# A running log-sum-exp in which the fp16 matmuls become fp32 row sums, PSUM-held carries and a checked fast path

## The chip, the cores and the metric

The kernel runs on one core of a Trainium2 chip. The metric is the device time of one execution in microseconds, as the median of several runs; 3 runs of the kernel before gave a median of 1262.75 us (1262.56 to 1262.97). The profile is one more execution, recorded instruction by instruction.

## The reference

```
B, S, D = 4, 4096, 4128
x = np.random.randn(B, S, D).astype(np.float32)

out[:, 0, :] = x[:, 0, :]
for t in range(1, S):
    mx = np.maximum(out[:, t-1, :], x[:, t, :])
    out[:, t, :] = mx + np.log(np.exp(out[:, t-1, :] - mx) + np.exp(x[:, t, :] - mx))
```

For every batch and column it is the logarithm of the running sum of exp(x) down the 4096 rows. Both kernels compute exp, a running sum, and the logarithm of it.

## The kernel before, in words

**Tiles.** A step takes 128 x r consecutive rows of one batch, all 4128 columns, as one tile `xt` with r consecutive rows on each of the 128 partitions. r is 3 (`R`), and 2 in one step of each batch (first in batch 0, last in the others): 11 steps per batch, 44 in all, 40 of them with r = 3. A tile of r = 3 is 6192 KB. Four tiles are in rotation (`bufs = 4`). `Step.load` (L132) and `Step.store` (L135) both issue on SP's queue: after the store of step s comes the load of step s + 3, which has to wait until the tile's previous content is stored.

**Chunks.** A step is cut into four chunks of 1024 columns (`CH`); the last one also has the 32 columns that are left. For each chunk:

- `exp` (L147, ScalarE) writes exp(x) as fp16 over the chunk.
- `later` (L155, VectorE) adds rows 1 and 2 of each partition into `sum`, as fp32r.
- `head` (TensorE) makes row 0 of each partition in a PSUM tile `pt`: the triangle `incl` times row 0 of all partitions, the strict triangle `excl_r` times `sum` (L167), and `pick` times the carry of the step before. A matmul has 512 columns (`MM`), so each is there twice.
- `stage(j)` takes the logarithm of `pt` for row j (L198, ScalarE), and then adds row j + 1 into `pt` by a matmul with the identity `ident`. The rows of one chunk run one after another; three chunks are at different stages at the same time, with three `pt` tiles.
- `keep` (L111, L112, VectorE), after the last row, writes the last 32 partitions of `pt` as two fp16 parts, the rounded value and the remainder, into `carry`. `pick` adds both parts of partition 127 in the next step.

The 32 left columns go the same way with a small tile `qt` and `carry_t` (`tail_head`, L203). `mm` records a matmul, at L97 where the weights change and at L101 where they are those of the matmul before; the built order has a weight load ahead of both.

**Order.** The whole schedule is written out by hand (`manual_schedule`): the loop over chunks at L229 gives `later` of the next chunk, then the stages of three chunks, the store at a step's end, `exp` two chunks ahead and `head` one chunk ahead. Each engine runs its instructions in the order in which they are written.

Of the kernel before, what the change touches and what calls it, by code (L numbers as in the profile page):

```python
# [6 lines left out]

FP32 = mybir.dt.float32
FP16 = mybir.dt.float16
FP32R = mybir.dt.float32r  # L10
ACT = mybir.ActivationFunctionType
P = 128
R = 3
CH = 1024
MM = 512
HI, LO = 96, 32


def _constants(nc, pool):


    def tri(base, name):
        t = pool.tile([P, P], FP16, name=name)
        nc.gpsimd.memset(t, 1.0)

        nc.gpsimd.affine_select(
            out=t, in_=t, pattern=[[1, P]], compare_op=mybir.AluOpType.is_ge,
            fill=0.0, base=base, channel_multiplier=-1,
        )
        return t  # L30

    def ones_where_zero(bases, step, name):
        t = pool.tile([P, P], FP16, name=name)
        nc.gpsimd.memset(t, 0.0)
        for base in bases:
            nc.gpsimd.affine_select(
                out=t, in_=t, pattern=[[step, P]], compare_op=mybir.AluOpType.not_equal,
                fill=1.0, base=base, channel_multiplier=1,
            )
        return t  # L40

    return (
        tri(0, "incl"),
        tri(-1, "excl"),
        ones_where_zero([0], -1, "ident"),
        ones_where_zero([-(HI + 31), -(LO + 31)], 0, "pick"),
    )


@with_exitstack  # L50
def kernel(
    ctx: ExitStack,
    tc: tile.TileContext,
    x: bass.AP,
    out: bass.AP,
):

    nc = tc.nc
    B, S, D = x.shape
    assert S % P == 0
    n_main = D // CH
    tail = D - n_main * CH
    t0 = n_main * CH
    last = n_main - 1

    nc.scalar.preload_act_table_set("natural_log_exp_and_others")
    consts = ctx.enter_context(tc.tile_pool(name="consts", bufs=1))
    incl, excl, ident, pick = _constants(nc, consts)

    bufs = 4
    xpool = ctx.enter_context(tc.tile_pool(name="xpool", bufs=bufs))
    cpool = ctx.enter_context(tc.tile_pool(name="cpool", bufs=1))
    pmain = ctx.enter_context(tc.tile_pool(name="pmain", bufs=3, space=bass.MemoryType.PSUM))
    ptail = ctx.enter_context(tc.tile_pool(name="ptail", bufs=2, space=bass.MemoryType.PSUM))

    carry = [cpool.tile([P, CH], FP16, name=f"carry{c}") for c in range(n_main)]
    carry_t = cpool.tile([P, tail], FP16, name="carry_t")
    for t in (*carry, carry_t):
        nc.vector.memset(t, 0.0)

    spool = ctx.enter_context(tc.tile_pool(name="spool", bufs=1))
    excl_r = consts.tile([P, P], FP32R, name="excl_r")
    nc.vector.tensor_copy(excl_r, excl)

    ctx.enter_context(tc.manual_schedule())  # L90

    held = [None]

    def mm(pt, w, rhs, start=False, stop=False):

        if held[0] is not w:
            nc.tensor.matmul(pt, lhsT=w, rhs=rhs, start=start, stop=stop, skip_group_check=True)  # L97
            held[0] = w
            return
        pe = nc.tensor  # L100
        pe.add_instruction(mybir.InstMatmult(  # L101
            name=nc.get_next_instruction_name(),
            ins=[pe.lower_ap(rhs), pe.lower_ap(w, for_matmul_weights=True)],
            outs=[pe.lower_ap(pt, opt=True)],
            start_tensor_calc=start, stop_tensor_calc=stop, ldweights=False,
            tile_size=(P, P), tile_position=(0, 0), bass_skip_group_check=True,
        ))

    def keep(cr, pt):

        nc.vector.tensor_copy(cr[HI:HI + 32, :], pt[HI:HI + 32])  # L111
        nc.vector.tensor_tensor(  # L112
            out=cr[LO:LO + 32, :], in0=pt[HI:HI + 32], in1=cr[HI:HI + 32, :],
            op=mybir.AluOpType.subtract,
        )

    class Step:


        def __init__(self, b, row, r):  # L120
            self.b, self.row, self.r = b, row, r
            self.first = row == 0

        def dram(self, t):
            rows = t[self.b, self.row:self.row + P * self.r, :]
# [2 lines left out]
        def load(self):  # L128
            full = xpool.tile([P, R, D], FP32, name="xt")
            self.xt = full[:, :self.r, :]  # L130
            self.half = self.xt.bitcast(FP16)
            nc.sync.dma_start(out=self.xt, in_=self.dram(x))  # L132

        def store(self):
# [2 lines left out]
    class Chunk:  # L137
        def __init__(self, step, c):
            self.t, self.c = step, c
            self.w = D - last * CH if c == last else CH  # L140

        def e(self, j, a, b):
            return self.t.half[:, j, 2 * self.c * CH + a:2 * self.c * CH + b]

        def exp(self):
            c0, w = self.c * CH, self.w
            nc.scalar.activation(  # L147
                self.t.half[:, :, 2 * c0:2 * c0 + w], self.t.xt[:, :, c0:c0 + w], ACT.Exp,
            )

        def later(self):

            if self.t.r == 3:
                self.sum = spool.tile([P, CH], FP32R, name="sum")
                nc.vector.tensor_tensor(  # L155
                    out=self.sum, in0=self.e(1, 0, CH), in1=self.e(2, 0, CH),
                    op=mybir.AluOpType.add,
                )

        def head(self):  # L160
            t = self.t
            pt = self.pt = pmain.tile([P, CH], FP32, name="pt")
            for s in range(0, CH, MM):
                mm(pt[:, s:s + MM], incl, self.e(0, s, s + MM), start=True)
            if t.r == 3:
                for s in range(0, CH, MM):
                    nc.tensor.matmul(  # L167
                        pt[:, s:s + MM], lhsT=excl_r, rhs=self.sum[:, s:s + MM],
                        start=False, stop=False, skip_group_check=True,
                    )  # L170
                held[0] = None
            else:
                for s in range(0, CH, MM):
                    mm(pt[:, s:s + MM], excl, self.e(1, s, s + MM))
            if not t.first:
                for s in range(0, CH, MM):
                    mm(pt[:, s:s + MM], pick, carry[self.c][:, s:s + MM])
            if self.c == last:
                self.tail_head()

        def tail_head(self):


            t, r = self.t, self.t.r
            full = ptail.tile([P, R, tail], FP32, name="qt")
            qt = self.qt = full[:, :r, :]
            to = lambda v, n: v.unsqueeze(1).to_broadcast([P, n, tail])
            for i in range(r):
                mm(qt[:, i:, :], incl, to(self.e(i, CH, CH + tail), r - i), start=i == 0)
            for i in range(1, r):  # L190
                mm(qt[:, :i, :], excl, to(self.e(i, CH, CH + tail), i))
            if not t.first:
                mm(qt, pick, to(carry_t, r))

        def stage(self, j):

            t, c, pt = self.t, self.c, self.pt
            nc.scalar.activation(t.xt[:, j, c * CH:(c + 1) * CH], pt, ACT.Ln)  # L198
            if j + 1 < t.r:
                for s in range(0, CH, MM):  # L200
                    mm(pt[:, s:s + MM], ident, self.e(j + 1, s, s + MM), stop=j + 2 == t.r)
                if c == last and j == 0:
                    nc.scalar.activation(t.xt[:, :, t0:D], self.qt, ACT.Ln)  # L203
                    keep(carry_t, self.qt[:, t.r - 1, :])
            else:
                keep(carry[c], pt)

    steps = []
    for b in range(B):
        n = S // P  # L210
# [3 lines left out]
        row = 0  # L214
# [2 lines left out]
            row += P * r  # L217
        assert row == S

    chunks = [Chunk(s, c) for s in steps for c in range(n_main)]  # L220
    ahead = bufs - 1
    for s in steps[:bufs]:
        s.load()
    stored = 0
    chunks[0].exp()
    chunks[1].exp()
    chunks[0].later()
    chunks[0].head()
    for g in range(len(chunks) + R - 1):  # L229
        if g + 1 < len(chunks):  # L230
            chunks[g + 1].later()
        for d in range(R - 1, -1, -1):
            if 0 <= g - d < len(chunks) and d < chunks[g - d].t.r:
                k = chunks[g - d]
                k.stage(d)
                if k.c == last and d + 1 == k.t.r:
                    k.t.store()
                    if bufs <= stored + ahead < len(steps):
                        steps[stored + ahead].load()
                    stored += 1  # L240
        if g + 2 < len(chunks):
            chunks[g + 2].exp()
        if g + 1 < len(chunks):
            chunks[g + 1].head()


# [28 lines left out]
```

## Time and profile before

| | before |
|---|---|
| median of 3 runs | 1262.75 us |
| profiled execution, span from first to last instruction | 1261.5 us |
| TensorE busy, matmuls | 661.2 us, 52% |
| VectorE busy | 647.7 us, 51% |
| ScalarE busy | 947.3 us, 75% |
| DMA queue of loads and stores, share of 16 engines | 99.4% |
| moved, mean rate | 541.44 MB, 429 GB/s |
| mean granted TensorE clock | 0.722 |

Busy time is the time in which an engine has an instruction of the program running, as a share of the span. In the lists of groups a line names the source line, the engine, the operation, its output and inputs by the program's names with partitions x elements and type, and the number of instructions; after the first bar stand the busy time in us and the mean of one in ns, and after the second bar the idle time of the engine just before them and what ended most of it. PE is TensorE, PEld its weight loads, DVE VectorE, ACT ScalarE, POOL GpSimd, SP SyncE, whose queue issues the DMAs. The rows of tenths cut the span into 40 slices: 9 is 90% or more; PEclk is the clock that TensorE was granted, in tenths of full speed.

### The profile page before, as it was taken

The page shows a single profiled execution, that of the slowest core. Times are in us where ns is not written, and L with a number is a line of the kernel's source. Part 1 is how long each engine was busy: PE and PEld are TensorE (multiplying, and loading weights), DVE is VectorE, ACT ScalarE, POOL GpSimd, SP SyncE. Part 2 cuts the span into 40 slices and gives each one's busy share as a digit, 9 for nine tenths or more (in the row PEclk, how much of TensorE's full clock was granted, in tenths as well). Part 3 has the DMA queues.
Part 4 walks back from the last instruction along what each step waited for, and adds up shares of the span by engine and source line. Part 5 has one row for each costly group of instructions (what it writes and reads, how often), then busy time and mean ns, then how long its engine had stood idle before and what let it go on. Part 6 is the DMA issues. An engine that isn't in the chain of part 4 may idle for free. (4 is left out here: it accounts for less than half of the span.)

```text
span 1261.5 us, 5926 instructions
## 1 busy us (share of the span) xinstructions
PE 661.2 (52%) x1948; PEld 236.7 (19%) x1948; DVE 647.7 (51%) x606; ACT 947.3 (75%) x733; POOL 2.2 (0%) x13
## 2 busy tenths in 40 slices
PE   3655545465555555555446554555534655544562
PEld 1222111122121111211112121111111221111120
DVE  2674445554555545545446545544544645544454
ACT  5997777777777777778669777777866977777784
POOL 0000000000000000000000000000000000000000
PEclk9987676766577776768757677766775767787666
DMA  9999999999999999999999999999999999999998
GB/s 410 410 437 434 429 430 437 431 430 431 440 430 431 430 439 430 431 433 431 438 433 435 428 432 438 432 430 431 434 435 430 435 427 436 434 434 429 437 416 346
DMA packets 12702, 541.44 MB, mean 429 GB/s; under 512 B 1408, under 2 KB 1408, under 8 KB 1408
## 3 DMA queue, kind: packets, MB, share of 16 engines
q1 hardware_dynamic: 12672, 541.07, 99.4%
q8 instruction: 15, 0.25, 0.1%
q14 instruction: 15, 0.12, 0.0%
HBM read 270.53 MB, written 270.53 MB: 429 GB/s over the span
## 5 line engine op out<-in xcount | busy, mean ns | idle before, releaser
L147 ACT ACTIVATE xt<-xt 128x3072 f16<-128x3072 f32 (+3 forms) x176 | 478.3, 2717 | 248.4 <-DMA xt<-in_x_dram 248.4
L198 ACT ACTIVATE xt<-pt 128x1024 f32<-128x1024 f32 x512 | 487.5, 1029 | 2.5 <-PE pt L101 0.7
L155 DVE TENSOR_TENSOR sum<-xt 128x1024 fp32r<-128x1024 f16 x160 | 196.0, 1225 | 531.2 <-ACT xt L147 406.7
L97 PE MATMUL pt<-xt,ident 128*128 128x512 f16 x176 | 82.9, 471 | 482.8 <-ACT xt L198 482.8
L111 DVE CAST carry<-pt 32x1024 f16<-32x1024 f32 x176 | 216.4, 1230 | 46.4 <-ACT xt L198 41.3
L101 PE MATMUL pt<-xt,ident 128*128 128x512 f16 x496 | 209.5, 495 | 28.4 <-ACT xt L198 28.1
L112 DVE TENSOR_TENSOR carry<-pt,carry 32x1024 f16<-32x1024 f32 x176 | 215.9, 1226 | 6.1
L167 PE MATMUL pt<-sum,excl_r 128*128 128x512 f32 x320 | 198.7, 716 | 0.0
L101 PEld LDWEIGHTS <-ident 128*128 128x128 f16 x496 | 52.4, 106 | 646.5 <-issue 636.1
L97 PE MATMUL pt<-xt,incl 128*128 128x512 f16 x176 | 95.7, 544 | 71.7 <-DVE carry L112 54.0
L167 PEld LDWEIGHTS pt<-sum,excl_r 128*128 128x128 f32 x320 | 95.4, 298 | 48.4 <-issue 31.1
L101 PE MATMUL pt<-xt,incl 128*128 128x512 f16 x176 | 99.2, 564 | 0.0
L97 PE MATMUL pt<-carry,pick 128*128 128x512 f16 x160 | 84.4, 528 | 0.0
L101 PE MATMUL pt<-carry,pick 128*128 128x512 f16 x160 | 79.4, 496 | 0.0
L97 PEld LDWEIGHTS <-incl 128*128 128x128 f16 x220 | 23.7, 108 | 192.7 <-DVE carry L112 167.0
L203 ACT ACTIVATE xt<-qt 128x96 f32<-128x96 f32 (+1 forms) x44 | 10.9, 249 | 46.3 <-PE pt L101 46.3
L97 PEld LDWEIGHTS <-pick 128*128 128x128 f16 x200 | 24.2, 121 | 67.0 <-issue 66.3
L101 PEld LDWEIGHTS <-incl 128*128 128x128 f16 x260 | 27.6, 115 | 12.7 <-issue 9.2
L97 PEld LDWEIGHTS <-ident 128*128 128x128 f16 x176 | 21.4, 122 | 30.3 <-issue 24.3
L101 PEld LDWEIGHTS <-pick 128*128 128x128 f16 x160 | 20.5, 128 | 2.4 <-issue 1.7
L111 DVE CAST carry_t<-qt 32x32 f16<-32x32 f32 x44 | 8.7, 197 | 13.7 <-ACT xt L203 13.5
L97 PE MATMUL qt<-xt,incl 128*128 128x96 f16 (+1 forms) x44 | 10.6, 240 | 0.0
(25 smaller groups left out, 79.8 us busy)
## 6 DMA issues: line engine op xcount, KB each, us to landing
xt<-in_x_dram SPq DMA_DIRECT2D x40, 6192.0 KB, 42.3
out_dram<-xt SPq DMA_DIRECT2D x40, 6192.0 KB, 28.1
xt<-in_x_dram SPq DMA_DIRECT2D x4, 4128.0 KB, 37.4
out_dram<-xt SPq DMA_DIRECT2D x4, 4128.0 KB, 29.7
```

The costliest lines, as they stand in the source:

```text
L97: nc.tensor.matmul(pt, lhsT=w, rhs=rhs, start=start, stop=stop, skip_group_check=True)
L101: pe.add_instruction(mybir.InstMatmult(name=nc.get_next_instruction_name(), ins=[pe.lower_ap(rhs), pe.lower_ap(w, for_matmul_weights=True) ...
L111: nc.vector.tensor_copy(cr[HI:HI + 32, :], pt[HI:HI + 32])
L112: nc.vector.tensor_tensor(out=cr[LO:LO + 32, :], in0=pt[HI:HI + 32], in1=cr[HI:HI + 32, :], op=mybir.AluOpType.subtract,)
L147: nc.scalar.activation(self.t.half[:, :, 2 * c0:2 * c0 + w], self.t.xt[:, :, c0:c0 + w], ACT.Exp,)
L155: nc.vector.tensor_tensor(out=self.sum, in0=self.e(1, 0, CH), in1=self.e(2, 0, CH), op=mybir.AluOpType.add,)
L167: nc.tensor.matmul(pt[:, s:s + MM], lhsT=excl_r, rhs=self.sum[:, s:s + MM], start=False, stop=False, skip_group_check=True,)
L198: nc.scalar.activation(t.xt[:, j, c * CH:(c + 1) * CH], pt, ACT.Ln)
L203: nc.scalar.activation(t.xt[:, :, t0:D], self.qt, ACT.Ln)
```

## The change

- exp(x) stays fp32, in place. VectorE makes the running sums of the r rows on each partition, in place (`sums`, r - 1 additions).
- The columns are three chunks of 1024 and a last one of 1056. For each of the first three a PSUM tile `base[c]` stays for the whole kernel. `head` adds the strict triangle `excl` times the partitions' totals (the last row of `sums`), in fp32; VectorE adds `base[c]` to all r rows in one instruction (`add`); `pass_on` then starts the next step's base with `pick` times the last row, so the carry needs no copy. For the last chunk the base is made in three tiles of 352 columns (two in rotation), from `carry` and the totals, and added piece by piece (`add_rest`); `add` copies the last 32 partitions to `carry`.
- One logarithm per chunk, over all r rows, from SBUF (`ln`).
- A range check: `total` adds up the final sums of each batch and chunk on partitions 96 to 127, `first` holds exp(-x) of the first rows, and all of it is compared with 2^40. Every engine reads the flag and branches: if the check fails, `_general` computes everything again by the reference's own steps, 4095 of them in a loop.
- All fp16 and fp32r tiles, the identity, `later`, `stage`, `keep` and `tail_head` are gone. The order is still written by hand.

Lines in the text on the changed kernel are its own (L112 sums, L124 and L126 head of the last chunk, L131 head, L137 add_rest, L144 carry copy, L147 add, L155 pass_on, L108 exp, L167 ln, L163 total, L249 to L256 `_general`).

```diff
+BUFS = 4
+HI = 96
+LIMIT = float(2 ** 40)
...
+    carry = cpool.tile([P, rest], FP32, name="carry")
...
+    base = [pkeep.tile([P, CH], FP32, name=f"base{c}") for c in range(3)]
...
         def exp(self):
-            c0, w = self.c * CH, self.w
-            nc.scalar.activation(
-                self.t.half[:, :, 2 * c0:2 * c0 + w], self.t.xt[:, :, c0:c0 + w], ACT.Exp,
-            )
-
-        def later(self):
-
-            if self.t.r == 3:
-                self.sum = spool.tile([P, CH], FP32R, name="sum")
+            rows = self.rows(0, self.t.r)
+            nc.scalar.activation(rows, rows, ACT.Exp)
+
+        def sums(self):
+            for j in range(1, self.t.r):
                 nc.vector.tensor_tensor(
-                    out=self.sum, in0=self.e(1, 0, CH), in1=self.e(2, 0, CH),
-                    op=mybir.AluOpType.add,
-                )
+                    out=self.row(j), in0=self.row(j - 1), in1=self.row(j), op=ALU.add)
 
         def head(self):
             t = self.t
...
+            own = self.row(t.r - 1)
+            if self.end:
+                self.base = []
+                for s in range(0, rest, sub):
+                    q = prest.tile([P, MM], FP32, name="q")
+                    self.base.append(q)
+                    if not t.first:
+                        nc.tensor.matmul(q[:, :sub], lhsT=pick, rhs=carry[:, s:s + sub],
+                                         start=True, stop=False, skip_group_check=True)
+                    nc.tensor.matmul(q[:, :sub], lhsT=excl, rhs=own[:, s:s + sub],
+                                     start=t.first, stop=True, skip_group_check=True)
+                    self.add_rest(s, q)
             else:
                 for s in range(0, CH, MM):
...
+                    nc.tensor.matmul(base[self.c][:, s:s + MM], lhsT=excl, rhs=own[:, s:s + MM],
+                                     start=t.first, stop=True, skip_group_check=True)
+
+        def add_rest(self, s, q):
+            t = self.t
+            rows = t.xt[:, :, self.a + s:self.a + s + sub]
+            nc.vector.tensor_tensor(
+                out=rows, in0=rows, in1=q[:, :sub].unsqueeze(1).to_broadcast([P, t.r, sub]),
+                op=ALU.add)
+
+        def add(self):
+            t = self.t
+            if self.end:
+                nc.vector.tensor_copy(carry[HI:P, :], self.row(t.r - 1)[HI:P])
+                return
+            rows = self.rows(0, t.r)
+            nc.vector.tensor_tensor(
+                out=rows, in0=rows, in1=base[self.c].unsqueeze(1).to_broadcast([P, t.r, CH]),
+                op=ALU.add)
+
+        def pass_on(self):
+            if self.end:
+                return
+            for s in range(0, CH, MM):
+                nc.tensor.matmul(base[self.c][:, s:s + MM], lhsT=pick,
+                                 rhs=self.row(self.t.r - 1)[:, s:s + MM],
+                                 start=True, stop=False, skip_group_check=True)
+
+        def total(self):
+            own = carry if self.end else base[self.c]
+            i = 4 * self.t.b + self.c
+            nc.vector.tensor_reduce(
+                out=part[HI:P, i:i + 1], in_=own[HI:P, :self.w], axis=AX.X, op=ALU.add)
+
+        def ln(self):
+            rows = self.rows(0, self.t.r)
+            nc.scalar.activation(rows, rows, ACT.Ln)
...
     chunks[0].exp()
     chunks[1].exp()
-    chunks[0].later()
+    chunks[0].sums()
     chunks[0].head()
...
+    for g, k in enumerate(chunks):
+        if not k.end:
+            chunks[g + 1].sums()
+        k.add()
+        k.pass_on()
+        if g + 2 < n:
             chunks[g + 2].exp()
...
+        k.ln()
+        if g and chunks[g - 1].t.last:
+            chunks[g - 1].total()
...
+        if k.end:
+            k.t.store()
+            if BUFS <= stored + BUFS - 1 < len(steps):
+                steps[stored + BUFS - 1].load()
+            stored += 1
+            if g + 1 < n:
+                chunks[g + 1].sums()
+        if g + 1 < n:
             chunks[g + 1].head()
+
+    chunks[-1].total()
+    nc.vector.tensor_reduce(out=every, in_=part, axis=AX.X, op=ALU.add)
+    q = prest.tile([P, MM], FP32, name="q")
+    nc.tensor.matmul(q[:1, :1], lhsT=every, rhs=ones, start=True, stop=True)
+    nc.vector.tensor_scalar(out=flag, in0=q[:1, :1], scalar1=LIMIT, scalar2=None, op0=ALU.is_le)
...
+    with ExitStack() as inner:
+        _fast(inner, tc, x, out, flag)
+    good = nc.values_load(flag, min_val=0, max_val=1, skip_runtime_bounds_check_because="a comparison gives 0 or 1")
+    with tc.If(good == 0, preferred_fallthrough_block=False):
+        with ExitStack() as inner:
+            _general(inner, tc, x, out)
```

## The prediction

> **What bounds the kernel now.** I read the page from the top: the busy shares, then the queues, then the costliest groups, and after them the timeline of TensorE. The first two say that no engine is full and the one DMA queue is.
>
> ```profile
> PE 661.2 (52%) x1948; PEld 236.7 (19%) x1948; DVE 647.7 (51%) x606; ACT 947.3 (75%) x733; POOL 2.2 (0%) x13
> ...
> PEclk9987676766577776768757677766775767787666
> DMA  9999999999999999999999999999999999999998
> ...
> q1 hardware_dynamic: 12672, 541.07, 99.4%
> ```
>
> 99.4% of 1261.5 us is 1254 us of transfers. The work is 40 steps of three row blocks and 4 steps of two, 42.7 three-block steps, so a full step has 1254 / 42.7 = 29.4 us. A change that leaves the bytes alone costs nothing while each step's work stays under that. The groups give the prices (mean ns of one stands after the bar).
>
> ```profile
> L147 ACT ACTIVATE xt<-xt 128x3072 f16<-128x3072 f32 (+3 forms) x176 | 478.3, 2717 | 248.4 <-DMA xt<-in_x_dram 248.4
> L155 DVE TENSOR_TENSOR sum<-xt 128x1024 fp32r<-128x1024 f16 x160 | 196.0, 1225 | 531.2 <-ACT xt L147 406.7
> L111 DVE CAST carry<-pt 32x1024 f16<-32x1024 f32 x176 | 216.4, 1230 | 46.4 <-ACT xt L198 41.3
> L112 DVE TENSOR_TENSOR carry<-pt,carry 32x1024 f16<-32x1024 f32 x176 | 215.9, 1226 | 6.1
> ```
>
> The list by shape has a smaller form of the last:
>
> ```profile
> L112 DVE TENSOR_TENSOR carry_t<-qt,carry_t 32x32 f16<-32x32 f32 x44 | 8.5, 193 | 1.5
> ```
>
> From the two L112 forms a VectorE operation costs (1226 - 193) / 992 = 1.04 ns per element per partition, on 0.16 us; half the partitions save nothing. ACT waits 248 us for loads: it has room. Last, two stretches of TensorE's timeline (start, length, instruction):
>
> ```profile
> 656.78 0.58 PE L97 MATMUL pt<-xt,ident 128*128 128x512 f16 x1 [10.27 <-ACT xt L198]
> ...
> 659.21 1.42 PE L167 MATMUL pt<-sum,excl_r 128*128 128x512 f32 x2
> 660.43 0.65 PE L97 MATMUL pt<-carry,pick 128*128 128x512 f16 x1
> 660.87 0.63 PE L101 MATMUL pt<-carry,pick 128*128 128x512 f16 x1
> ```
>
> ```profile
> 674.53 0.38 PE L97 MATMUL pt<-xt,ident 128*128 128x512 f16 x1 [1.18 <-ACT xt L198]
> 674.75 0.38 PE L101 MATMUL pt<-xt,ident 128*128 128x512 f16 x1
> ...
> 677.08 0.81 PE L167 MATMUL pt<-sum,excl_r 128*128 128x512 f32 x2
> 677.72 0.39 PE L97 MATMUL pt<-carry,pick 128*128 128x512 f16 x1
> ```
>
> A matmul's slot is the time to the next start. At full clock an f16 slot is 0.22 us (674.53 to 674.75), and an fp32r slot 0.32 us (677.08 to 677.72, two), 0.10 more because its weights are not loaded ahead. At half clock they are 0.44 and 0.61. The clock is half after a 10 us pause.
>
> **The change, part by part.** The f16 products go, and with them all of TensorE's and VectorE's old work. ScalarE has the same elements: per step four exps (three of 2.77 us and one of 2.89, by shape) and four logarithms of the same shapes, 22.4 us, beside other work. The bytes are equal but for 66 KB.
>
> VectorE per step: the row sums, 6 x 1.23 and 2 x 1.26; three adds of a PSUM base to 3 x 1024 elements, 1.226 + 2048 x 1.04 ns = 3.36 us each; three adds for the rest, 3 x 352 elements, 1.26 each; the carry copy, 32 x 1056. The copy's nearest row is L111, 1.23 us, so 1.26. Sum 25 us: under 29.4 by itself. The Trainium skill (VectorE: DVE Perf Modes, "The perf-mode tier table") has an fp32 copy within SBUF at twice the rate; by it the copy would be 0.7 us and the total some 25 us less; no row here shows such a copy.
>
> TensorE: the built order has 780 fp32 matmuls, 18 in a step (12 of 512 columns, 6 of 352), each with its own weights. No fp32 product stands in the trace. The low bound is the fp32r slot, 0.32 us at full clock, if an fp32 product goes through the array once. The high bound comes from the old kernel's own arithmetic: keep() needs two f16 pieces to carry one fp32 value, and here both operands are unrounded, so two pieces by two pieces, four passes, 4 x 0.32 = 1.28 us. I take four passes of 0.22 with two weight loads of 0.10, 1.08 us: fp32r is the row for rounded operands, and this change drops the rounding. The Trainium skill (FP8 and Floating Point Precision, "TensorE Precision Notes") also counts four passes for true fp32, against the one that the fp32r row shows; by that rule alone the total is near 1630 us at the least, by the row alone 1262.
>
> The clock: durations run from 0.38 us (full) to 0.63 (half), and the six costly f16 groups of 512 columns average 0.485, so (0.485 - 0.38) / 0.25 = 42% of them ran at half clock, a mean price 1.42 times the full one. The changed kernel pauses TensorE for 3.6 us at each add, and fills the rest; I take the same 1.42. So m = 1.08 x 1.42 = 1.53 us per 512 columns. A 352-column one is 0.69 x 0.88 + 0.20 = 0.81 against 1.08, 0.75 m.
>
> Now the order, which decides. In PE's queue pass_on of chunk g stands ahead of head of chunk g + 1. pass_on waits for add(g) on VectorE (it reads the row that add writes), and add(g + 1) waits for head(g + 1). So TensorE and VectorE take turns, in a chain with no slack, where L155 and L111 before ran beside the matmuls. The legs, with 0.05 us from DVE to PE (the trace: 604.41 to 604.46) and 0.3 from the last matmul's slot to DVE (tail 0.17 and wake 0.12):
> - chunks 0 to 1 and 1 to 2: add 3.36, 0.05, four matmuls 4m, 0.3, twice;
> - chunk 2 to 3: add 3.41, two matmuls 2m, six short ones 4.5m with two of the three rest adds beneath them, then 0.3 and the last rest add 1.26;
> - chunk 3 to the next step: carry copy 1.30, two sums 2.54 (placed behind the copy, so nothing hides them), 0.05, then the longer of head, 2m + 0.3, and the next chunk's sums, 2.5, which stand ahead of add in DVE's queue.
>
> A step is 16.3 + 14.5m + max(2m + 0.3, 2.5). With m = 1.53 it is 16.3 + 22.2 + 3.4 = 41.9 us, against 29.4 of transfers: the DMA no longer sets the end. A two-block step is 4.85 shorter (three adds by 1.07, one sum 1.27, the rest add 0.37): 37.0. Twelve short matmuls are missing at the heads of the batches, -14 us. Before the first sum 15 us pass (first load landed at 13.2, one exp 1.9), and 2 us of fill; at the end a logarithm and the last store, 14 us, take the place of 7 us of the last leg: +24. 40 x 41.9 + 4 x 37.0 - 14 + 24 = 1834 us of span. The median of before, 1262.75, lies 1.25 above the profiled span, so 1835 us.
>
> At no cost: what SP waits for. A load waits for the store before the last one, which lands 28.1 us after its issue even with the queue full as now, and was issued 41.9 us earlier. At nothing, too, the four small loads of the first row, issued on ACT's queue before the 13.2 us wait for x, and their exp (about 0.25 us, ACT has 19 us free per step); if ACT were full they would cost that. The range check (a reduction 1.3 us, two small operations 0.4, a one-column matmul, the flag read by each engine) lies beneath the last store's 12 us; without that cover 3 to 5 us. Every branch waits on that flag, with nothing queued behind it.
>
> **The rivals.**
> - *The clock stays full.* For it: TensorE's busy share would be about 60% against 52%, and its bursts are longer. Against it: a 3.6 us pause per chunk, where 2.7 us (678.5 to 681.2) were followed by half clock at 683. m = 1.08: step 34.5, total 40 x 34.5 + 4 x 29.7 - 10 + 24 = 1513 us.
> - *One pass (the other side: not slower).* fp32 at the fp32r slot: m = 0.32 x 1.42 = 0.45, step 16.3 + 6.5 + 2.5 = 25.3, under 29.4, and the transfers set 1262 us as before. The point of decision is m = 0.73, where 16.3 + 14.5m + 2.5 = 29.4. For it: the fp32r row is the only 4-byte row. Against: its operands were rounded.
> - *Half clock throughout*: m = 2.16, step 52.2, total 2282 us. For it: stretches such as 656 to 671 at 0.5. Against: PEclk nowhere stays at 5.
> - *The general path runs too*, thousands of serial steps of at least 1.4 us: over 5.9 ms more. The check's sum for normal inputs is near 4096 x 1.65 x 16512 columns x 32 lanes = 3.6e9, against 1.1e12. It doesn't.
>
> **How the numbers follow.** Likeliest is the chain with a clock as before, 0.66, from 1631 us (m = 0.88 x 1.42 = 1.25) to 2039 (m = 1.28 x 1.42 = 1.82). Full clock 0.17; one pass 0.06; half clock 0.08; the general path 0.01; 0.02 for a small gain in a bound that stays the transfers, since the last store's tail could shrink. The range 1450 to 2050 leaves out one pass, half clock, the general path and the low end of full clock, about 0.19. Slower by over 0.2% (what a measurement of this kernel tells from no change) 0.92, within 0.06, faster 0.02.
>
> **What would show it.** Right: DMA share near 65 to 75%; PE and DVE idle in turns, add (L147) waiting for PE L131 and pass_on (L155) for DVE L147, both near 3 us or more each time; L147 at 3.36 us; 512-column fp32 slots of 1.1 and 2.1 us; the chain by PE and DVE, not DMA. Wrong: the queue at 99% and ACT waiting for loads as now (one pass), PEclk at 9 (full clock), L112 or L147 well off 1.23 and 3.36, or rows of L249 to L256 (general path).

## The result, and the profile after

The changed kernel takes 1710.9 us (median of four runs, 1693.4 to 1726.0), against 1262.65. The forecast was 1835 us in a range of 1450 to 2050. The execution in the profile is the longest and slowest of the four (1726.0 us, a span of 1724.3), and the ratio of 1.350 [1.344, 1.357] is taken without it, so that what is read from the trace of after is about 1% long. The four runs order by the clock that TensorE was granted (0.715, 0.717, 0.723 and 0.728 for 1726, 1712, 1710 and 1693 us).

The page after, parts 1 to 4, to be read beside the same rows of before:

```profile
PE 1042.7 (60%) x1562; PEld 421.3 (24%) x1562; DVE 1046.0 (61%) x664; ACT 934.9 (54%) x355; POOL 1.1 (0%) x9
...
PEclk9767676676687677676768667667676866766866
DMA  9678778778777778777769877876786987777535
...
q1 hardware_dynamic: 12672, 541.07, 74.7%
...
PE 50%; DVE 26%; ACT 12%; issue 10%; DMA 1%; ACTq 0%
```

The queue has fallen from 99.4% to 74.7%, and three quarters of the chain that ended last are TensorE and VectorE, with 1% of DMA. No engine is over 61%. Two engines that are 60% and 61% busy, with the chain going through both, make one suspect turns. The list of waits has the turns by name (time in total, times, longest):

```profile
PE base L155 <- DVE xt L147: 442.3, 132, 3.4
DVE xt L147 <- PE base L131: 377.0, 132, 5.3
DVE xt L137 <- PE q L126: 257.8, 88, 6.2
PE base L131 <- issue: 178.8, 38, 5.5
```

TensorE waits for every one of the 132 adds, 3.35 us each (442.3 / 132), before pass_on, and VectorE waits before every add for head. The last line is the pause before the head of a step's first chunk, which the profile puts down to nothing; an experiment below shows that it is for the row sums. One turn in the timeline, first VectorE's, then TensorE's:

```profile
806.37 3.35 DVE L147 TENSOR_TENSOR xt<-xt,base 128x3072 f32<-128x3072 f32 x1 [4.20 <-PE base L131]
809.64 2.55 DVE L112 TENSOR_TENSOR xt<-xt 128x1056 f32<-128x1056 f32 x2
816.46 3.35 DVE L147 TENSOR_TENSOR xt<-xt,base 128x3072 f32<-128x3072 f32 x1 [4.28 <-PE base L131]
```

```profile
809.78 3.78 PE L155 MATMUL base<-xt,pick 128*128 128x512 f32 x4 [3.45 <-DVE xt L147]
813.35 3.07 PE L131 MATMUL base<-xt,excl 128*128 128x512 f32 x4
```

From add to add it is 10.1 us: 3.35 of add, and eight records of matmuls. Each fp32 matmul stands as two records (x4 for the two pieces of 512 columns). From the groups by shape, the operations that the prediction had to price:

```profile
L147 DVE TENSOR_TENSOR xt<-xt,base 128x3072 f32<-128x3072 f32 x120 | 402.5, 3354 | 335.1 <-PE base L131 335.1
L112 DVE TENSOR_TENSOR xt<-xt 128x1024 f32<-128x1024 f32 x252 | 304.6, 1223 | 19.4 <-ACT xt L108 13.9
L137 DVE TENSOR_TENSOR xt<-xt,q 128x1056 f32<-128x1056 f32 x120 | 148.7, 1254 | 247.0 <-PE q L126 247.0
L144 DVE COPY carry<-xt 32x1056 f32<-32x1056 f32 x44 | 31.1, 706 | 1.5
```

Over all full steps of this trace the mean time from one chunk's add to the next is 9.4 us for the first chunk, 9.5 for the second, and 20.3 from the third to the next step's first: 39.2 us for a step.

### The profile page after: what moved, and what is told of

Its sections match the earlier page's. It is cut to its first block, busy times and chain, and to the rows that moved or that the text cites. A ratio compares the mean times of both kernels' runs of the same rounds, so it can differ in the third digit from the quotient of the medians.

```text
span 1724.3 us, 4771 instructions
## 1 busy us (share of the span) xinstructions
PE 1042.7 (60%) x1562; PEld 421.3 (24%) x1562; DVE 1046.0 (61%) x664; ACT 934.9 (54%) x355; POOL 1.1 (0%) x9
## 3 DMA queue, kind: packets, MB, share of 16 engines
q1 hardware_dynamic: 12672, 541.07, 74.7%
## 4 chain that ended last, share of the span: by engine, by line
PE 50%; DVE 26%; ACT 12%; issue 10%; DMA 1%; ACTq 0%
PE base L155 27%; DVE xt L147 25%; PE base L131 22%; ACT xt L167 6%; ACT xt L108 6%; PE q L124 1%; DVE xt L137 1%; DMA xt<-in_x_dram 1%; PE q L126 1%; DVE xt L112 0%; DVE carry L144 0%; DVE part L162 0%; PE q L219 0%; DVE every L217 0%; DVE flag L220 0%
## 5 line engine op out<-in xcount | busy, mean ns | idle before, releaser
L167 ACT ACTIVATE xt<-xt 128x3072 f32<-128x3072 f32 (+3 forms) x176 | 476.4, 2707 | 763.1 <-PE base L155 685.0
L155 PE MATMUL base<-xt,pick 128*128 128x512 f32 x528 | 459.8, 1021 | 442.3 <-DVE xt L147 442.3
L147 DVE TENSOR_TENSOR xt<-xt,base 128x3072 f32<-128x3072 f32 (+1 forms) x132 | 430.0, 3257 | 377.0 <-PE base L131 377.0
L131 PE MATMUL base<-xt,excl 128*128 128x512 f32 x528 | 395.0, 892 | 215.7 <-issue 178.8
L108 ACT ACTIVATE xt<-xt 128x3072 f32<-128x3072 f32 (+3 forms) x176 | 473.3, 2690 | 11.3 <-DMA xt<-in_x_dram 11.3
L112 DVE TENSOR_TENSOR xt<-xt 128x1024 f32<-128x1024 f32 (+1 forms) x336 | 410.1, 1231 | 26.8 <-ACT xt L108 19.7
L137 DVE TENSOR_TENSOR xt<-xt,q 128x1056 f32<-128x1056 f32 (+1 forms) x132 | 159.2, 1220 | 257.8 <-PE q L126 257.8
L155 PEld LDWEIGHTS base<-xt,pick 128*128 128x128 f32 x528 | 142.1, 297 | 709.4 <-DVE xt L147 582.8
L131 PEld LDWEIGHTS base<-xt,excl 128*128 128x128 f32 x528 | 157.1, 307 | 446.6 <-issue 423.7
L126 PE MATMUL q<-xt,excl 128*128 128x352 f32 x264 | 124.3, 562 | 1.1 <-DVE xt L137 1.1
L124 PE MATMUL q<-carry,pick 128*128 128x352 f32 x240 | 119.1, 584 | 4.7 <-DVE xt L137 2.5
L124 PEld LDWEIGHTS q<-carry,pick 128*128 128x128 f32 x240 | 60.2, 264 | 83.1 <-issue 55.5
L126 PEld LDWEIGHTS q<-xt,excl 128*128 128x128 f32 x264 | 61.9, 236 | 45.4 <-issue 22.6
L144 DVE COPY carry<-xt 32x1056 f32<-32x1056 f32 x44 | 31.1, 706 | 1.5
```

The source lines that it names most:

```text
L108: nc.scalar.activation(rows, rows, ACT.Exp)
L112: nc.vector.tensor_tensor(out=self.row(j), in0=self.row(j - 1), in1=self.row(j), op=ALU.add)
L124: nc.tensor.matmul(q[:, :sub], lhsT=pick, rhs=carry[:, s:s + sub], start=True, stop=False, skip_group_check=True)
L126: nc.tensor.matmul(q[:, :sub], lhsT=excl, rhs=own[:, s:s + sub], start=t.first, stop=True, skip_group_check=True)
L131: nc.tensor.matmul(base[self.c][:, s:s + MM], lhsT=excl, rhs=own[:, s:s + MM], start=t.first, stop=True, skip_group_check=True)
L137: nc.vector.tensor_tensor(out=rows, in0=rows, in1=q[:, :sub].unsqueeze(1).to_broadcast([P, t.r, sub]), op=ALU.add)
```

## The experiments

The theory: TensorE and VectorE take turns, so the length of fp32 matmuls and of adds is summed, and TensorE's pauses during the adds also pull its clock down, which makes its turns longer. The rivals are these: the volume of the fp32 matmuls is the bound whatever the order; VectorE's own work is; the clock does nothing, or all. A step or a leg (from one add to the next) is the mean over the full steps of a trace, as above.

**Head ahead of pass_on.**

```diff
         k.add()
+        if not k.end:
+            chunks[g + 1].head()
         k.pass_on()
...
-        if g + 1 < n:
+        if k.end and g + 1 < n:
             chunks[g + 1].head()
```

> In PE's queue the head of the next chunk is moved ahead of pass_on of this one (for the first three chunks of a step); no instruction is added or taken away. Taking turns (the theory): head no longer waits behind an add that it doesn't need, so it runs beside add. VectorE's 25 us per step and TensorE's 16.5 units of 0.86 to 1.4 us (14 to 23 us) are then side by side, both under the transfers' 29.4, and the time is 1262 to 1310 us, with the queue above 95%. Volume (the rival: the fp32 matmuls' sum at the granted clock is the bound, wherever it stands): the same work, so 1690 to 1730 us. Clock alone (second rival: only the half clock costs): the pauses get shorter, so some gain, but with the chain left about 1350 to 1500 us.

Measured 1353.1 us, 1.072 [1.070, 1.074]: 358 us less with the same instructions. Volume is out as the bound of the changed kernel. The forecast of 1262 to 1310 was missed by 43 us, and the time lies at the edge of what the second rival gave (1350 to 1500), so this run alone doesn't part the turns from the clock. TensorE's wait for the add has fallen from 442.3 to 65.7 us, and the waits name what took its place:

```profile
DVE xt L112 <- ACT xt L108: 251.8, 90, 13.4
```

The sums now wait for exp, since exp stands in ScalarE's queue behind a logarithm that waits for pass_on (376.7 us, L167 behind L155). The granted clock rose from 0.715 to 0.848.

**One pass.** The matmuls read only the upper halves of the sums and carries, as bf16, with the weights in bf16 too (one of the edits):

```diff
-                    nc.tensor.matmul(base[self.c][:, s:s + MM], lhsT=excl, rhs=own[:, s:s + MM],
+                    nc.tensor.matmul(base[self.c][:, s:s + MM], lhsT=excl, rhs=self.upper(s, MM),
```

> The same order with matmuls that read only the upper halves (bf16) of the fp32 sums and carries, and bf16 weights, so one pass; the lower halves are left out of the base. Taking turns: a leg is add 3.35, hand-overs 0.1 and four slots of 0.22 to 0.44 us, 5.0 us, less than VectorE's own 5.9 (add and two sums), so the chain has slack and the transfers set the time: 1262 to 1290 us. Hand-overs and VectorE (rival: the turns cost by VectorE's work and the waits, not by the length of the matmuls): above 1600 us.

Measured 1266.1 us, 1.0026 [1.0016, 1.0036], with the queue at 99.2%. A matmul is now one record and not two, and the slots of 512 columns, the time from one start to the next, are 0.38 to 0.43 us: by the slots of before (0.22 and 0.44) this is the half clock, all through the trace. So the order of the change costs almost nothing when a matmul is this short, even at half clock, and VectorE's 1034.6 us of work fit under the transfers. It is the length of the fp32 matmuls within the turns that sets the time, not the hand-overs. This is the second rival of the prediction, made true by the edit.

**Spare matmuls in the pauses.** First with one PSUM tile for the rest's two buffers (two of the edits):

```diff
+FILL, FILL_END = 8, 12
...
         def pass_on(self):
+            for _ in range(FILL_END if self.end else FILL):
+                nc.tensor.matmul(rests[:, 1, sub:MM], lhsT=excl, rhs=fill_x,
+                                 start=False, stop=False, skip_group_check=True)
```

> After each head eight spare fp32 matmuls of 160 columns (2.1 us at full clock) run into unused columns of PSUM while add has its turn, and twelve (3.2 us) at the end of a step; their result is used nowhere. Taking turns at a clock that the pauses pull down: the pauses shrink from 3.45 to about 1.4 us, the clock stays full, a leg is 3.35 + 0.1 + 3.7 = 7.2 instead of 9.4 us, a step about 30.4 instead of 39.2, and the time 1345 us (1300 to 1420), although TensorE has some 60% more matmuls. Volume: more matmuls, so more than 1711, up to 2100 us. Turns with a clock that the load doesn't move: the spares delay pass_on at half clock, 1711 to 1760 us.

Measured 1590.0 us, 1.259 [1.257, 1.261], clock 0.902. Faster than the change, by 121 us, but far from 1345. Its first two legs are 7.15 us each as forecast, its third 21.7 instead of 20.3: the edit had put the rest's two buffers into one tile, and each rest matmul then waited for the add of the one before (L127 behind L140, 105.6 us). With two tiles (`rests[0]`, `rests[1]`, nothing else changed):

> The spare matmuls again, with the two small PSUM tiles of the rest kept apart, since in the kernel before they were one tile and each rest matmul waited for the add of the one before (20.3 us became 21.7 from the third add to the next step, at a higher clock). Taking turns, with the clock as the larger part of the loss: legs of 7.15 us as measured there, and from the third add to the next step 15.5 to 18 us, so a step of 30 to 32 and 1310 to 1400 us in all. If the clock is not what the pauses cost: not below 1590.

Measured 1356.8 us, 1.075 [1.073, 1.076]. The page of this kernel:

```profile
PE 1092.9 (81%) x4730; PEld 725.7 (54%) x4730; DVE 1044.0 (77%) x666; ACT 934.4 (69%) x355; POOL 1.1 (0%) x9
...
PEclk9999999999999999999999999999999999999998
```

Three times the matmul records, work that nobody uses, and 354 us less. The clock is 0.996, the legs 7.14, 7.15 and 16.2 us, a step 30.5. TensorE still waits for 131 adds, but 1.25 us each time (164.0 / 131) instead of 3.35. So of the 448 us that the change lost, 354 went with the clock, and the turns at full clock cost the other 94. This is the clock's share in this order only: another order alone, at a clock of 0.848, had given back 358.

**The row sums of the first chunk, then of the others.** In two runs `sums` returns at once for chunk 0, or for all but chunk 0, so that these sums are left out.

> The row sums of each step's first chunk are left out (88 additions less 4, 1.22 us each, 103 us of VectorE's work). They are the ones that the chain waits for, between the carry copy and head. Taking turns: 2.4 us less per step, but the next chunk's sums (2.5 us) are then beside head, so the whole 2.4 is gained: 44 x 2.4 = 100 us, about 1610 us. Volume of matmuls: no change, 1690 to 1730 us.

Measured 1529.6 us, 1.211 [1.204, 1.217], 181 us less for 103 us of work left out, and 80 below the forecast. The third leg fell from 20.3 to 16.3 us, by more than the sums. In the trace of after the step's first head begins 2.65 us behind the carry copy, and from the copy's end to the next add are 6.3 us, of sums and head. Here head begins 2.2 us before the copy ends, right behind the rest matmuls; the pause of 4.65 us before it is gone, and only the next chunk's sums (2.5) stand between copy and add. So the sums had held back head as well, which the forecast left out. The other two legs are 0.3 and 0.5 us shorter, at a clock of 0.756.

> The row sums of the second to fourth chunk of each step are left out (252 additions, some 310 us of VectorE's work, three times what the kernel without the first chunk's sums left out). They run while TensorE has its turn. Taking turns: nothing gained, 1690 to 1730 us. VectorE's own work as a cost (rival): up to 310 us less, about 1400 us; a part of it if the order in VectorE's queue matters.

Measured 1751.6 us, 1.388 [1.386, 1.390]: three times as much VectorE work left out, and no gain but 41 us more, at a clock of 0.700. VectorE's share fell to 42%. So what stands beside TensorE's turn was free, as the theory has it. The 41 us were not expected; a leg is 0.1 to 0.5 us longer at the lower clock, and why the clock was lower stays open.

**What is left when the turns go.** Two heads early, and each logarithm and store one chunk later:

```diff
         k.add()
+        if k.c < 2:
+            chunks[g + 1].head()
         k.pass_on()
...
-        k.ln()
+        if g:
+            p = chunks[g - 1]
+            p.ln()
+            if p.end:
+                p.t.store()
...
-        if g + 1 < n:
+        if k.c >= 2 and g + 1 < n:
             chunks[g + 1].head()
```

> Head is moved ahead of pass_on for the first two chunks of a step only (the third's head, with its rest adds, stays behind pass_on), and each logarithm, with the store behind it, is issued one chunk later, so that ScalarE's next exp doesn't stand behind a logarithm that waits for pass_on (the idle time before the sums in the kernel with every head moved: 251.8 us behind exp). Taking turns: the two turns are gone and so is the wait that took their place; legs 5.8 and 6 to 7 us, the rest about 16, a step under 29.4, and the transfers set 1263 to 1290 us. If the fp32 matmuls' volume has a share that no order hides: 1330 to 1360, as with every head moved.

Measured 1358.4 us, 1.076 [1.074, 1.077]. This is a miss, and it lies where the rival of volume had put it (1330 to 1360). The first two legs are 5.8 us, as expected, and the wait for exp is gone, but the third leg is 19.3, not 16. VectorE's timeline shows where:

```profile
818.66 3.35 DVE L147 TENSOR_TENSOR xt<-xt,base 128x3072 f32<-128x3072 f32 x1
826.78 2.44 DVE L137 TENSOR_TENSOR xt<-xt,q 128x1056 f32<-128x1056 f32 x2 [4.77 <-PE q L126]
829.58 1.25 DVE L137 TENSOR_TENSOR xt<-xt,q 128x1056 f32<-128x1056 f32 x1 [0.36 <-PE q L126]
830.87 0.71 DVE L144 COPY carry<-xt 32x1056 f32<-32x1056 f32 x1
831.61 1.23 DVE L112 TENSOR_TENSOR xt<-xt 128x1024 f32<-128x1024 f32 x1
```

VectorE idles 4.77 us after the third add, and then makes the next step's sums behind the copy, while TensorE waits for them. They can be made in that hole:

```diff
             chunks[g + 2].exp()
+            if k.c == 2:
+                chunks[g + 2].sums()
...
-            if g + 1 < n:
-                chunks[g + 1].sums()
```

> Head ahead of pass_on for the first two chunks, the logarithms where the change put them, and the next step's first sums moved from behind the carry copy to behind the third add, where VectorE waits 4.8 us for the rest matmuls. Taking turns: the last leg, 19.3 us in the kernel with late logarithms, loses the two sums (2.5 us) and the wait for head behind them (1.5), since head then follows the rest matmuls on TensorE. A step of 26.8 us and more of clock is under 29.4: the transfers set the time, 1263 to 1285 us, without a matmul fewer than in the change. If the fp32 matmuls' volume has a floor of its own: about 1350.

> The same with each logarithm and store one chunk later. If ScalarE's exp behind a waiting logarithm still matters, this is the faster of the two, 1263 to 1285 us against 1290 to 1330; if not, both are alike and this one ends some 3 us later, as its last store starts later.

Without the late logarithms the kernel took 1344.2 us, 1.065 [1.061, 1.069], again a miss and near the 1350 of the rival: the second leg is 8.5 us, with L112 again behind exp (133.0 us). With them it took 1276.7 us, 1.010 [1.009, 1.012], as forecast. Its page:

```profile
q1 hardware_dynamic: 12672, 541.07, 98.6%
...
DMA 57%; DVE 17%; ACT 15%; PE 6%; issue 4%; SPq 0%; ACTq 0%; DVEq 0%
```

The transfers lead the chain again, with every fp32 matmul of the change in place, so volume has no floor of its own above this; and the clock is 0.875, lower than the 0.996 of the spare matmuls, which took 1357 us, so the clock alone is not the cause either. The early heads gave 358 us by themselves; the late logarithms added to them gave nothing (1358), the earlier sums without late logarithms little (1344), and both together 76 more. Each edit but the last had moved the wait to another place. The 14 us that are left above the kernel before were not looked into.

**The range check.** The kernel with two early heads and late logarithms, without the check:

> The kernel with two heads early and late logarithms, without the range check, its loads of the first rows, its sums and the branch to the general path. The prediction held the check to be hidden beneath the last store: 0 to 3 us less than the same kernel with it. If the branch waits for more than the store (rival): 5 to 15 us less.

Measured 1347.7 us, 1.067 [1.066, 1.068], so the check costs 10.6 us there (1358.4 - 1347.7), more than the 0 to 3 expected and within the rival's 5 to 15. But only part of it is at the end, where the rival had it: from the last store's issue (1341.29) to the end of the span (1356.5) are 15.2 us, against 11.9 without (1334.66 to 1346.6). The rest lies at the ends of the batches, where sixteen sums of 1.23 us stand in VectorE's queue (the longest first leg is 7.07 us with them, 5.67 without): the adds of the two traces move 3 to 4 us apart at each of the first three ends, and drift in between.

## Why the prediction was right, step by step

The mechanism held: the chain of turns is there, the order was read correctly, the transfers no longer set the end, and the price of VectorE's operations was right to 0.01 us (3.35 for 3.36, 1.22 for 1.23, 1.25 for 1.26). The time came out 124 us lower than the sum, and that it was no further off is in part luck: the two factors of a matmul's price were off by 20% and 17% in opposite directions. With the first corrected alone the prediction's sum would give some 1610 us, with the second alone some 2020. These terms were mis-sized:

- **The matmul at full clock**: taken as 1.08 us, four passes with two weight loads shown. In fill2 a leg at full clock is 7.15 us; without add and hand-over (3.41) and the tail (0.3) four matmuls take 3.44, 0.86 each. That is what four slots of 0.215 take with the weight loads hidden, near the f16 slot of 0.22 and below the low end (0.88) of the prediction's estimate. So the slots named as a sign, 1.1 and 2.1 us, are 0.86 and 1.71. The fp32r slot of 0.32 us, the nearest row of the trace of before, was no guide. The Trainium skill (FP8 and Floating Point Precision, "TensorE Precision Notes") has four passes for true fp32, and the 0.86 us agree with it, though the trace shows two records and not four.
- **The clock's factor**: taken as 1.42 from the mean of the old f16 matmuls. A leg of 9.43 us leaves 5.72 us for four matmuls, 1.43 each, so the factor is 1.43 / 0.86 = 1.66. This error went the other way; m came out as 1.43 against 1.53. Part of it is a reading: 0.485 us is busy time over number, in which overlapping records count once, and the means of the rows give 0.511, a factor of 1.53. The rest is that the mean clock was as before (0.715 against 0.722), but the half-clock stretches caught the matmuls: 535 slots of 0.84 to 0.86 us stand in the trace against 111 of 0.42 to 0.44.
- **The carry copy**: 1.26 us from the row of a copy out of PSUM; measured 0.71. The estimate that the prediction worked out from a page of the Trainium skill (VectorE: DVE Perf Modes, "The perf-mode tier table") was 0.7, and the trace agrees.
- With these three the sum of a step is 39.6 us instead of 41.9, and 39.2 was measured. Over 40 steps the 2.7 us are 108, about the difference between the summed span (1834) and the profiled one (1724.3).
- **The rival with a full clock** was priced at 1513 us. fill2 is that case, and takes 1357, since the same two terms, matmul and copy, are too high: 0.22 x 14.5 + 0.6 = 3.8 us a step of 34.5, and 30.5 was measured.
- **The range check** was counted as hidden beneath the last store. Its sums at the ends of the batches were left out of the working altogether: 19.8 us of VectorE's work, part of it on the chain.
- Two slips had no effect: the rows L155 and L112 compare 128 partitions with 32, a quarter and not half, and 4095 steps of 1.4 us are 5.7 ms, not 5.9.

By its own prices the prediction had put 322 of 572 us on the clock (1835 against 1513); the runs have 354 of 448. It named the pauses as what speaks against a full clock, but took the factor from the old kernel, as if it were fixed. In the runs it moves with the pauses: with them filled the clock is 0.996, and with the best order, and no filling, 0.875.

## What to carry to other kernels

When two engines at about 60% each wait for one another and the transfers have idle time, read the order in each queue before the amount of work: moving matmuls ahead of others that they do not depend on gave 358 us here, with nothing computed less. After each such move look for the wait that takes its place; here it took three moves, one for each engine, until the transfers were the bound again. And price a matmul with the clock that its pauses will leave it.

## What the runs showed of the hardware

An fp32 matmul of 512 columns stands in the trace as two records of 0.43 us at full clock (0.85 at half), each with its own weight load (0.19 us) hidden: 0.86 and 1.71 us.

TensorE's clock changes in the traces of before, after, fill2 and early_head only at marks 3.413 us apart, or multiples of that. By the records of these four traces it goes from half to full after a stretch of that length in which matmul records cover 80% or more (all 325 rises follow one with at least 78%, and none above 82% was without a rise), and from full to half after one covered by less than about 45% (the highest before a fall is 51%, the lowest that kept the full clock 41%). The seven other traces with such marks agree but for half-clock stretches of up to 85% without a rise.

A pause of 3.35 us leaves one of the two stretches that it touches at 51% or less (1 - 1.675 / 3.413); one of 1.25 us alone leaves at least 63%, and fill2, with one stretch at 43% and the others at 53% or more, kept the full clock to its end. The Trainium skill (TensorE: Matmul & The Clock Gate, "Part 1: The HAM clock gate") has the two states and the length of 3.4 us, but lets the clock fall after an idle stretch. Here it fell after stretches that were up to half busy. The measurement decides, and this is why useless matmuls made the kernel faster.
